# A depthwise convolution over time, moved onto the tensor engine as products over (phase, channel) rows

## The chip, the cores and the metric

The kernel runs on one core of a Trainium2 chip as a single launch. A core has a tensor engine (PE, with PEld for its weight loads), a vector engine (DVE), a scalar engine (ACT), a general engine (POOL) and a queue engine (SP) that starts the DMAs; each runs its own list of instructions in order, and they wait for each other by semaphores. Arrays live in SBUF as 128 partitions by so many elements, and the results of PE land in PSUM, from which DVE and ACT read them. The metric is device time in microseconds (us), the median of several runs.

## The reference

A decoder trunk of four layers works on 512 prompt tokens and 8 sample tokens of 1024 channels. Layer i uses token mixer i mod 3, so that the third layer alone is a convolution module; every mixer and every feed-forward block has a norm before and after it and is added to the running state x.

```
def conv_mixer(h, hist, w_in, b_in, w_dw, b_dw, ln_g, ln_b, w_out, b_out):
    a = h @ w_in + b_in                                  # 1024 -> 2048
    u = a[..., :D_MODEL] * jax.nn.sigmoid(a[..., D_MODEL:])
    uh = jnp.concatenate([hist, u], axis=1)              # 30 tokens of history, zeros for the prompt
    c = conv_general_dilated(uh, w_dw[:, None, :], feature_group_count=D_MODEL, ...) + b_dw   # 31 taps
    mu, var = mean and variance of c over the channels
    z = (c - mu) * lax.rsqrt(var + LN_EPS) * ln_g + ln_b
    y = jax.nn.silu(z) @ w_out + b_out
    return y, uh[:, -CONV_HIST:]
```

The depthwise convolution is the line that matters: each channel of a token is the sum of 31 weights, one per step back in time, times the same channel of the token and the 30 before it.

## The kernel before, in words

All activations are kept with channels on partitions: eight blocks of 128 channels, each a row of 520 tokens (8 sample tokens and 512 of the prompt). The tokens are worked on in two column groups, CA (columns 0 to 263, the sample tokens and 256 of the prompt) and CB (264 to 519). Full products (`mm3`, lines 393 to 395) are three reduced-precision passes over a high and a low part of activations (`mh`, `ml`) and weights (`wh`, `wl`): three PE instructions per 128 inputs. A weight block of 128 outputs is one 512 KB DMA from SP's queue (L354), one ACT cast to `wh` (L364) and one DVE subtraction to `wl` (L365).

The convolution stage (`_conv`) walks over m = 0 to 3; each m makes two blocks of 128 channels (2m and 2m+1), for CA and then for CB. `in_products` issues 48 PE instructions for the first block of a pair, 48 for the second, and after each 48 takes up to 32 steps (`FILL_CONV`) of a generator called `fill`. Then `evac` multiplies the sums by the norm's factor (L1184, L1186, on DVE), takes the sigmoid (L1185, ACT) and writes u (L1190, L1193, DVE) into `conv_u`, where each block has 30 zero tokens ahead of 512.

The generator holds the depthwise convolution of the two blocks of the m before. `depthwise` divides the 31 taps by the table `CONV_TAPS`: for blocks 0 to 5, over all 512 tokens, 15 on DVE (L1272, L1274, each a multiply and add in place over `y`), 11 on ACT as products (L1263) that POOL adds up (L1268), and 5 on PE (L1249) with a diagonal 128 by 128 matrix that ACT makes for each tap (L1248). The three partial sums meet on DVE (L1278, L1279). Blocks 6 and 7 come last and are done in halves of 256 tokens (14, 7 or 8, and the rest on PE). `sum_blocks` (L1293) then makes the sums over the channels with a matrix of ones, `layer_norm` (L1306 to L1321) subtracts the mean, squares, forms the factor (`rstat`, L179 to L186), multiplies by it, applies the SiLU and splits into `mh` and `ml`, and `linear_out` multiplies by `conv_w_out`. The norm of CA runs beside the taps of blocks 6 and 7 for the second half. `conv_out` (L1230 to L1232) transposes the last 30 tokens of u and the sample tokens and writes them out.

The program text gives one order per engine; a static scheduler then reorders instructions by its own estimates, with the limits of the tile pools (so many buffers of a name) and the dependencies. At the start of the stage the previous block's tail is still in progress: for CB, DVE makes `xt` (L234), POOL adds it to x (L239), ACT and DVE split it into `mh` and `ml` (L318, L319), and the products of m = 0 for CB wait for that.

## Times and the profile before

| | us |
|---|---|
| median of 3 runs | 2636.73 (2634.72 to 2644.44) |
| profiled execution | 2639.77 |
| its span on the core | 2638.0 |
| mean granted TensorE clock, share of full speed | 0.973 |
| PE busy over the span | 2490.6 (94%) |
| DVE busy | 1764.8 (67%) |
| ACT busy | 1326.9 (50%) |
| POOL busy | 503.1 (19%) |

The rest of the profiled execution, 1.8 us, lies outside the span. Busy shares are averages over the whole program; the stage of the convolution is a small part of it, from about 1513 us of the span (the first product of `conv_w_in`) to about 1776 (the last one of `conv_w_out` for CA is close by). In rows of products a record begins when its first column enters and its end is modelled, so that records overlap: the time one product costs is the step from one start to the next.

### The profile page before, as it was taken

How to read it: one execution, taken by the hardware profiler on the slowest of the kernel's cores; microseconds unless marked ns; L12 is line 12 of the kernel's file. 1: busy time of each engine (PE TensorE's matmuls, PEld its weight loads, DVE VectorE, ACT ScalarE, POOL GpSimd, SP SyncE). 2: the span in 40 equal slices, each digit the busy share in tenths (PEclk: the TensorE clock that was granted, in tenths of full speed). 3: DMA queues.
4: the chain of work that ended last, by engine and by line, in shares of the span. 5: the costliest groups of instructions: out<-in, count | busy, mean ns of one | idle time of the engine just before them, and what ended most of it. 6: DMA issues, size and time to landing. Idle time of an engine off the chain costs nothing. (4 is left out here: it accounts for less than half of the span.)

```text
span 2638.0 us, 50548 instructions
## 1 busy us (share of the span) xinstructions
PE 2490.6 (94%) x20200; PEld 2437.6 (92%) x20200; DVE 1764.8 (67%) x3063; ACT 1326.9 (50%) x2484; POOL 503.1 (19%) x667
## 2 busy tenths in 40 slices
PE   7999999999999999899999996679999998999998
PEld 7899999999999998799999984579999998999998
DVE  5745555677887777676555599977646456746464
ACT  6634334566666556554433464466534236644342
POOL 3100002233233332310000256622000005200002
PEclk8999999999999999999999998789999998999999
DMA  4575553444444444446555320025646442556451
GB/s 144 161 215 158 152 152 108 128 125 140 137 140 135 122 137 139 133 143 186 157 153 150 98 73 17 18 65 138 193 142 184 120 124 65 158 165 174 136 160 57
DMA packets 653432, 349.76 MB, mean 133 GB/s; under 512 B 14864, under 2 KB 649729, under 8 KB 652909
## 3 DMA queue, kind: packets, MB, share of 16 engines
q1 hardware_dynamic: 648996, 338.10, 44.8%
q0 software_dynamic: 1232, 6.06, 0.8%
q8 instruction: 159, 2.61, 0.4%
q10 hardware_dynamic: 2969, 2.37, 0.4%
q14 instruction: 76, 0.62, 0.1%
HBM read 331.87 MB, written 20.68 MB: 134 GB/s over the span
## 5 line engine op out<-in xcount | busy, mean ns | idle before, releaser
L393 PE MATMUL mm<-mh,wh 128*128 128x264 f32 (+1 forms) x4544 | 1310.6, 290 | 34.9 <-DVE u L1184 19.7
L394 PE MATMUL mm<-ml,wh 128*128 128x264 f32 (+1 forms) x4544 | 1295.5, 285 | 6.5 <-DVE ml L319 6.0
L395 PE MATMUL mm<-mh,wl 128*128 128x264 f32 (+1 forms) x4544 | 1291.3, 285 | 1.1 <-DVE wl L365 1.1
L364 ACT CAST wh<-raw 128x1024 fp32r<-128x1024 f32 (+1 forms) x557 | 574.0, 1036 | 655.6 <-PE mm L394 391.7
L393 PEld LDWEIGHTS mm<-mh,wh 128*128 128x128 f32 x4544 | 864.9, 191 | 41.9 <-DVE u L1184 21.6
L365 DVE TENSOR_TENSOR wl<-raw,wh 128x1024 fp32r<-128x1024 f32 (+1 forms) x557 | 691.9, 1246 | 284.1 <-ACT wh L364 281.8
L394 PEld LDWEIGHTS mm<-ml,wh 128*128 128x128 f32 x4544 | 868.0, 191 | 12.4 <-DVE ml L319 10.1
L395 PEld LDWEIGHTS mm<-mh,wl 128*128 128x128 f32 x4544 | 866.6, 191 | 1.6 <-DVE wl L365 1.5
L393 PE MATMUL mm<-h,wh 128*128 128x264 f32 (+1 forms) x1408 | 399.9, 284 | 1.0 <-DVE pr L1159 0.8
L394 PE MATMUL mm<-h,wh 128*128 128x264 f32 (+1 forms) x1408 | 399.0, 283 | 1.0 <-DVE h L422 0.9
L395 PE MATMUL mm<-h,wl 128*128 128x264 f32 (+1 forms) x1408 | 399.1, 283 | 0.0
L222 POOL TENSOR_TENSOR acc<-acc,sq 128x264 f32<-128x264 f32 (+1 forms) x90 | 78.5, 872 | 1389.9 <-ACT sq L221 1386.8
L393 PEld LDWEIGHTS mm<-h,wh 128*128 128x128 f32 x1408 | 266.4, 189 | 2.2 <-issue 1.0
L394 PEld LDWEIGHTS mm<-h,wh 128*128 128x128 f32 x1408 | 266.5, 189 | 1.7 <-DVE h L422 1.4
L395 PEld LDWEIGHTS mm<-h,wl 128*128 128x128 f32 x1408 | 266.3, 189 | 0.1
L419 DVE TENSOR_TENSOR u<-mm,r 128x264 f32<-128x264 f32 (+1 forms) x176 | 74.9, 425 | 84.9 <-PE mm L395 84.8
L1274 DVE SCALAR_TENSOR_TENSOR y<-conv_u,vec,y 128x512 f32<-128x512 f32 (+1 forms) x136 | 131.3, 1001 | 0.0
L239 POOL TENSOR_TENSOR x<-x,xt 128x264 f32<-128x264 f32 (+1 forms) x111 | 98.0, 906 | 96.3 <-DVE xt L234 94.6
L1268 POOL TENSOR_TENSOR tapa<-tapa,tapp 128x512 f32<-128x512 f32 (+1 forms) x76 | 105.5, 1388 | 18.3 <-DVE y L1279 12.5
L456 DVE TENSOR_TENSOR y<-mm,y 128x264 f32<-128x264 f32 x64 | 24.0, 429 | 124.5 <-PE mm L395 124.5
L417 DVE TENSOR_TENSOR g<-mm,r 128x264 f32<-128x264 f32 (+1 forms) x176 | 74.8, 425 | 41.6 <-PE mm L395 37.7
L937 ACT ACTIVATE x<-x,own 128x256 f32<-128x256 f32 (+1 forms) x128 | 62.6, 490 | 63.4 <-DVE own L936 62.4
(223 smaller groups left out, 2688.2 us busy)
## 6 DMA issues: line engine op xcount, KB each, us to landing
raw<-in_w_ffn_in_dram SPq DMA_DIRECT2D x352, 512.0 KB
raw<-in_w_qkv_dram SPq DMA_DIRECT2D x72, 512.0 KB
raw<-in_w_ffn_out_dram SPq DMA_DIRECT2D x64, 512.0 KB
skv<-in_cache_swa_g_dram SPq DMA_DIRECT2D x32, 512.0 KB
raw<-in_w_ffn_out_dram SPq DMA_DIRECT2D x32, 384.0 KB
out_dram<-tm SPq DMA_DIRECT2D x32, 256.0 KB
raw<-in_conv_w_in_dram SPq DMA_DIRECT2D x16, 512.0 KB
skv<-in_cache_swa_g_dram SPq DMA_DIRECT2D x16, 256.0 KB
```

Of the source, the lines that this page charges most:

```text
L222: (eng or nc.vector).tensor_add(post[c], post[c], sq)
L239: self.added = nc.gpsimd.tensor_add(xb, xb, t)
L364: whi = nc.scalar.copy(wh, raw)
L365: self.parted = whi, nc.vector.tensor_sub(wl, raw, wh.bitcast(F32))
L393: nc.tensor.matmul(ps, wh[:, k, :], mh, start=first, stop=False)
L394: nc.tensor.matmul(ps, wh[:, k, :], ml, start=False, stop=False)
L395: nc.tensor.matmul(ps, wl[:, k, :], mh, start=False, stop=last)
L417: nc.vector.tensor_mul(g, pg[2 * i], rr[c])
L419: nc.vector.tensor_mul(u, pg[2 * i + 1], rr[c])
L937: nc.scalar.activation(pc, pc, AF.Exp, scale=-1.0, bias=stat[:, lay, 0, c:c + 1], accum_out=stat[:, lay, 1, c:c + 1])
L1268: nc.gpsimd.tensor_add(a2, ap, pr)
L1274: nc.vector.scalar_tensor_tensor(yb, win(ub, t), wd[:, b, t:t + 1], yb, op0=ALU.mult, op1=ALU.add)
```

## The change

The taps of DVE, ACT and POOL go; PE does all 31 for all eight blocks. A block's u is stored by phase, that is by token number mod 4 (`cu`: phase p, then 128 tokens n, with token 4n + p), and POOL copies it (`to_phases`) into four tiles, one for each group q of 32 channels, whose 128 rows are 4 phases by 32 channels; eight zero columns stand ahead. A weight matrix of 128 by 128 then holds, for a step of m columns (4m tokens) back, the taps between each of the four input phases and each of the four output phases; nine such steps cover the 31 taps. A group is therefore nine products of 128 columns summed in PSUM, a block 4 x 9 = 36. The matrices are cut out of one tile `dg` of 128 x 36 x 32 per group, which DVE makes (L1241) by multiplying an identity pattern by the weights of `w2`; `w2` and the biases `b2` are laid out once by POOL (`depthwise_setup`). Sixteen instructions of 32 partitions by 2 x 64 bring a block from PSUM to `y`, with the bias, back on its channel rows but with the prompt tokens of each column group by phase; for blocks 0 to 5 all are ACT's, for blocks 6 and 7 every second one is DVE's. The multiplication by the norm's factor puts the tokens back in order (two instructions for CA instead of one). `CONV_FILL` says how many steps of six products are taken after each 48 products. The taps of the last m and all channel sums now come after the loop.

```diff
-FILL_CONV = 32
-CONV_TAPS = [(15, 11), (14, 7), (14, 8)]
+CONV_FILL = {(1, CB): 3, (2, CA): 3, (2, CB): 3, (3, CA): 3, (3, CB): 2}
...
-            if fill:
-                for _ in range(FILL_CONV):
-                    next(fill, None)
+            for _ in range(n_fill):
+                next(fill, None)
...
-        nc.gpsimd.memset(u[:, :, 0:H], 0.0)
...
+        self.u2 = [lp.tile([128, 4, 8 + 128], F32, name=f"conv_u2{i}") for i in range(4)]
+        self.depthwise_setup(lp)
...
+        fill = chain(*(self.depthwise(lp, b) for b in range(NB)))
...
-                            nc.vector.scalar_tensor_tensor(u[:, b, H:H + 256], a[:, NS:], self.v(R_BIN, b), g[:, NS:],
-                                                           op0=ALU.add, op1=ALU.mult)
...
+                            ub[b] = lp.tile([128, 4, 128], F32, tag="cu", name=self.n("cu"), bufs=4)
+                        o, n0 = (NS, 0) if lo == 0 else (0, 64)
+                        phases = lambda x: x[:, o:].rearrange("c (n p) -> c p n", p=4)
+                        nc.vector.scalar_tensor_tensor(ub[b][:, :, n0:n0 + 64], phases(a), self.v(R_BIN, b), phases(g),
+                                                       op0=ALU.add, op1=ALU.mult)
+                        if lo > 0:
+                            self.to_phases(b, ub[b])
+
+                self.in_products(ww, c, rr, evac, fill, CONV_FILL.get((m, c), 0))
             self.flush()
-            for _ in fill:
-                pass
-            if m < 3:
-                fill = chain(*(self.depthwise(lp, b, 0, SEQ, CONV_TAPS[0]) for b in (2 * m, 2 * m + 1)))
-            if m > 1:
-                for s in sums:
-                    for _ in range(2):
-                        next(s)
+        for _ in fill:
+            pass
+        for s in sums:
+            for _ in range(7):
+                next(s)
         self.conv_out(j)
         norm = [self.layer_norm(c, s) for c, s in zip((CA, CB), sums)]
-        for _ in chain(*(self.depthwise(lp, b, 0, 256, CONV_TAPS[1]) for b in (6, 7))):
+        for _ in norm[0]:
             pass
...
+    def depthwise_setup(self, lp):
+
+        nc = self.nc
+        self.w2 = lp.tile([128, NB, 4, 36], F32, name="conv_w2")
+        self.b2 = lp.tile([128, NB, 4], F32, name="conv_b2")
+        self.id32 = lp.tile([128, 32], F32, name="conv_id")
+        nc.vector.tensor_reduce(self.id32, self.ident.rearrange("p (b k) -> p k b", b=4), axis=AX.X, op=ALU.add)
+        nc.gpsimd.memset(self.w2, 0.0)
+        for u2 in self.u2:
+            nc.gpsimd.memset(u2[:, :, 0:8], 0.0)
+        for p in range(4):
+            for q in range(4):
+                pp, pq = slice(32 * p, 32 * p + 32), slice(32 * q, 32 * q + 32)
+                nc.gpsimd.tensor_copy(self.w2[pp, :, q, 5 - p:36 - p], self.vec[pq, :, R_DW:R_DW + 31])
+                nc.gpsimd.tensor_copy(self.b2[pp, :, q], self.vec[pq, :, R_BDW])
+
+    def to_phases(self, b, ub):
+
+        nc, u2 = self.nc, self.u2[b % 4]
+        for q in range(4):
+            for p in range(4):
+                nc.gpsimd.tensor_copy(u2[32 * p:32 * p + 32, q, 8:], ub[32 * q:32 * q + 32, p, :])
+        nc.gpsimd.tensor_copy(self.ul[:, b, :].rearrange("c (n p) -> c p n", p=4), ub[:, :, 120:128])
+
+    def depthwise(self, lp, b):
...
+        for q in range(4):
+            d = lp.tile([128, 36, 32], F32, tag="dg", name=self.n("dg"), bufs=6)
+            nc.vector.tensor_mul(d, self.id32[:, None, :].to_broadcast([128, 36, 32]),
+                                 self.w2[:, b, q, :, None].to_broadcast([128, 36, 32]))
+            dg.append(d)
+        ps = self.psum()
+        for q in range(4):
+            for m in range(9):
+                nc.tensor.matmul(ps[:, q * 128:q * 128 + 128], dg[q][:, 32 - 4 * m:36 - 4 * m, :].rearrange("p e c -> p (e c)"),
+                                 u2[:, q, 8 - m:136 - m], start=m == 0, stop=m == 8, skip_group_check=True)
+                if (q * 9 + m) % 6 == 5:
+                    yield
+        yb = self.y[:, b, NS:].rearrange("c (h p n) -> c h p n", h=2, p=4)
+        for q in range(4):
+            for s in range(4):
+                src = ps[32 * s:32 * s + 32, q * 128:q * 128 + 128].rearrange("c (h n) -> c h n", h=2)
+                dst, bias = yb[32 * q:32 * q + 32, :, 3 - s, :], self.b2[32 * s:32 * s + 32, b, q:q + 1]
+                if b >= 6 and s % 2:
+                    nc.vector.tensor_scalar(dst, src, bias, None, op0=ALU.add)
+                else:
+                    nc.scalar.activation(dst, src, AF.Identity, bias=bias)
```

Removed with it (not shown): the old `depthwise`, its halves for blocks 6 and 7, and `self.u`. After the scheduler, three places read as follows. A row is the instruction's number on its engine, its line, the operation, and tile names with their numbers; xN is a run of equal rows. Line numbers are each kernel's own (L239 before is L238 after).

On POOL, at the start of the stage, before:

```order
202 L239 TENSOR_TENSOR x<-x,xt_18721 128x264
203 L239 TENSOR_TENSOR x<-x,xt_18726 128x264
204 L1170 MEMSET conv_u 128x8x30
205 L177 MEMSET sd_19013 128x1
206 L239 TENSOR_TENSOR x<-x,xt_18899 128x256
207 L239 TENSOR_TENSOR x<-x,xt_18904 128x256
208 L239 TENSOR_TENSOR x<-x,xt_18909 128x256
209 L239 TENSOR_TENSOR x<-x,xt_18914 128x256
210 L239 TENSOR_TENSOR x<-x,xt_18919 128x256
```

And after, where the rows from 204 on are the two kinds of memset and sixteen pairs of copies, and these are the last two pairs:

```order
237 L1223 COPY conv_w_18796<-vec 32x8x31
238 L1224 COPY conv_b_18797<-vec 32x8
239 L1223 COPY conv_w_18796<-vec 32x8x31
240 L1224 COPY conv_b_18797<-vec 32x8
241 L176 MEMSET sd_19057 128x1
242 L238 TENSOR_TENSOR x<-x,xt_18943 128x256
243 L238 TENSOR_TENSOR x<-x,xt_18948 128x256
244 L238 TENSOR_TENSOR x<-x,xt_18953 128x256
245 L238 TENSOR_TENSOR x<-x,xt_18958 128x256
```

The 37 rows of the setup stand ahead of the eight additions to x of column group CB.

On DVE, at the same place (with what each row waits for), before:

```order
1808 L365 TENSOR_TENSOR wl_19173<-raw_19170,wh_19172 128x1024 [waits DMAHW3_49,Activation_49]
1809 L333 TENSOR_TENSOR acc_2643_18867<-acc_2643_18867,sq_18875 128x264 [waits DVE_49]
1810 L184 RECIPROCAL rd_18895<-sd_18891 128x2 [waits Activation_49]
1811 L333 TENSOR_TENSOR acc_2643_18867<-acc_2643_18867,sq_18878 128x264 [waits DVE_49]
1812 L333 TENSOR_TENSOR acc_2643_18867<-acc_2643_18867,sq_18881 128x264 [waits DVE_49]
1813 L234 SCALAR_TENSOR_TENSOR xt_18899<-mm_18890,vec,y 128x256 [waits PE_49]
1814 L333 TENSOR_TENSOR acc_2643_18867<-acc_2643_18867,sq_18884 128x264 [waits DVE_49]
1815 L234 SCALAR_TENSOR_TENSOR xt_18904<-mm_18890,vec,y 128x256
```

And after:

```order
1808 L331 TENSOR_TENSOR acc_2643_18911<-acc_2643_18911,sq_18916 128x264 [waits DVE_49,Activation_49]
1809 L183 RECIPROCAL rd_18939<-sd_18935 128x2 [waits Activation_49]
1810 L363 TENSOR_TENSOR wl_19253<-raw_19250,wh_19252 128x1024 [waits DMAHW3_49]
1811 L331 TENSOR_TENSOR acc_2643_18911<-acc_2643_18911,sq_18919 128x264 [waits DVE_49]
1812 L1241 TENSOR_TENSOR dg_19434<-conv_id,conv_w_18796 128x1152 [waits Pool_49]
1813 L331 TENSOR_TENSOR acc_2643_18911<-acc_2643_18911,sq_18922 128x264 [waits DVE_49]
1814 L233 SCALAR_TENSOR_TENSOR xt_18943<-mm_18934,vec,y 128x256 [waits PE_49]
1815 L331 TENSOR_TENSOR acc_2643_18911<-acc_2643_18911,sq_18925 128x264 [waits DVE_49]
```

The first weight matrix (L1241, row 1812) waits for POOL and stands ahead of the first `xt` of CB (L234 before, L233 after).

On PE, at the end of the stage, before (L1249 are taps of block 7's second half; L1293 the channel sums of CB; L393 the first product of `linear_out`):

```order
12340 L1249 MATMUL mm_20596<-conv_u,dg_20612 128x256
12341 L1249 MATMUL mm_20596<-conv_u,dg_20615 128x256
12342 L1249 MATMUL mm_20596<-conv_u,dg_20618 128x256
12343 L1249 MATMUL mm_20596<-conv_u,dg_20621 128x256
12344 L179 MATMUL mm_20655<-ones,acc_3014_20624 128x2 x2
12345 L179 MATMUL mm_20655<-ones,acc_3014_20624 8x2
12346 L1293 MATMUL mm_19971<-y,ones 128x256 x3
12347 L186 MATMUL mm_20655<-ident,rd_20663 128x128 x2
12348 L186 MATMUL mm_20655<-ident,rd_20663 128x8
12349 L393 MATMUL mm_20812<-mh,wh_20802 128x264
12350 L393 MATMUL mm_20813<-mh,wh_20808 128x264
12351 L393 MATMUL mm_20916<-mh,wh_20906 128x264
```

And after (L1247 are the last three of block 7's four groups of products; L1282 the sums, L1272 the transposes of `conv_out`):

```order
12297 L1247 MATMUL mm_20551<-conv_u_18795,dg_20545 128x128 x9
12298 L1247 MATMUL mm_20551<-conv_u_18795,dg_20547 128x128 x9
12299 L1247 MATMUL mm_20551<-conv_u_18795,dg_20549 128x128 x9
12300 L1282 MATMUL mm_20606<-y,ones 128x264 x7
12301 L1282 MATMUL mm_20614<-y,ones 128x256 x7
12302 L1272 MATMUL mm_20623<-ident,conv_us 8x128 x4
12303 L1272 MATMUL mm_20629<-ident,conv_us 8x128 x4
12304 L1272 MATMUL mm_20637<-ident,conv_ul 32x128 x4
12305 L1272 MATMUL mm_20643<-ident,conv_ul 32x128 x4
12306 L1282 MATMUL mm_20606<-y,ones 128x264
12307 L1282 MATMUL mm_20614<-y,ones 128x256
12308 L178 MATMUL mm_20682<-ones,acc_2832_20651 128x2 x2
```

The taps of blocks 4 to 7 (24 + 36 + 36 + 36 products) end in one run, then come the sums with all but the last block, the transposes, and the sums' last product; the products of CB's half no longer stand between the sums of CA and the norm.

## Rows read from the trace of the kernel before

**Rows 1.** Windows of the conv stage: busy time per engine, PEclk, DMA share, GB/s.
```profile
1513.40:1550.40 37.00, 33.66 (x271) 32.44 (x269) 32.76 (x72) 27.72 (x58) 8.84 (x14) 1.00 0.46 129
1550.40:1724.90 174.50, 120.52 (x669) 97.20 (x670) 174.04 (x212) 82.72 (x169) 118.98 (x86) 0.85 0.06 17
```

**Rows 2.** Waits, 1550.4 to 1724.9: us in total, times, longest us.
```profile
PE mm L393 <- DVE u L1184: 19.7, 3, 9.4
...
PE mm L1249 <- DVE conv_u L1193: 9.7, 2, 9.0
```

**Rows 3.** Lines by form, DVE, 1550.4 to 1743.3: busy us, mean ns.
```profile
L1274 DVE SCALAR_TENSOR_TENSOR y<-conv_u,vec,y 128x512 f32<-128x512 f32 x84 | 103.4, 1260 | 0.0
...
L1306 DVE SCALAR_TENSOR_TENSOR y<-mm,y 128x264 f32<-128x264 f32 x8 | 2.9, 424 | 0.6 <-PE mm L1293 0.6
```

**Rows 4.** Timeline, DVE: start us, us, line, count.
```profile
1553.78 15.34 DVE L1274 SCALAR_TENSOR_TENSOR y<-conv_u,vec,y 128x512 f32<-128x512 f32 x9
...
1637.41 0.73 DVE L1274 SCALAR_TENSOR_TENSOR y<-conv_u,vec,y 128x512 f32<-128x512 f32 x1
...
1642.94 2.29 DVE L365 TENSOR_TENSOR wl<-raw,wh 128x1024 fp32r<-128x1024 f32 x1
```

**Rows 5.** Timeline, POOL, same stretch.
```profile
1553.65 14.92 POOL L1268 TENSOR_TENSOR tapa<-tapa,tapp 128x512 f32<-128x512 f32 x9
```

**Rows 6.** Timeline, PE: products of 264 and of 256 tokens.
```profile
1513.44 0.28 PE L393 MATMUL mm<-mh,wh 128*128 128x264 f32 x1
...
1516.12 0.29 PE L394 MATMUL mm<-ml,wh 128*128 128x264 f32 x1
...
1540.73 0.28 PE L393 MATMUL mm<-mh,wh 128*128 128x256 f32 x1
...
1542.71 0.28 PE L395 MATMUL mm<-mh,wl 128*128 128x256 f32 x1
```

**Rows 7.** Timeline, PE: products with a fresh weight tile each.
```profile
22.74 2.04 PE L615 MATMUL mm<-bands,h 128*128 128x144 f32 x16
```

**Rows 8.** Windows around such products, at two clocks.
```profile
19.40:21.40 2.00, 2.00 (x10) 2.00 (x10) 0.01 (x1) 0.36 (x2) 0.00 (x0) 0.50 0.24 72
22.80:24.70 1.90, 1.90 (x17) 1.78 (x16) 0.88 (x2) 1.76 (x4) 0.00 (x0) 1.00 0.34 95
```

**Rows 9.** Lines, PE, 1513.4 to 1550.38.
```profile
L393 PE MATMUL mm<-mh,wh 128*128 128x264 f32 (+1 forms) x80 | 23.0, 288 | 0.0
```

**Rows 10.** One line, POOL: ns min/median/max.
```profile
L975 POOL COPY oth<-own x128: 180/186/1251, 535.5 to 1058.1; 32x4 f32<-32x4 f32 x128
```

**Rows 11.** Lines by form, POOL, whole span.
```profile
L1085 POOL TENSOR_TENSOR skv<-skv,y 128x1152 f32<-128x1152 f32 x16 | 43.0, 2707 | 24.0 <-DMA skv<-scr 23.4
```

**Rows 12.** Timeline, POOL, 1512 to 1536.
```profile
1515.46 0.29 POOL L1170 MEMSET conv_u<- 128x240 f32 x1
...
1524.19 3.15 POOL L239 TENSOR_TENSOR x<-x,xt 128x256 f32<-128x256 f32 x4 [8.40 <-DVE xt L234]
```

**Rows 13.** Timeline, DVE, 1520 to 1527.
```profile
1523.62 0.48 DVE L234 SCALAR_TENSOR_TENSOR xt<-mm,vec,y 128x256 f32<-128x256 f32 x1
```

**Rows 14.** One line, ACT: ns min/median/max.
```profile
L1248 ACT ACTIVATE dg<-ident,vec x68: 384/387/402, 1520.5 to 1731.7; 128x128 f32<-128x128 f32 x68
```

**Rows 15.** One line, DVE: ns min/median/max.
```profile
L1159 DVE TENSOR_TENSOR pr<-mm,vec x16: 269/273/275, 1180.8 to 1223.2; 128x120 f32<-128x120 f32 x16
```

**Rows 16.** Timeline, PE, 1722 to 1745.4.
```profile
1723.70 1.25 PE L1293 MATMUL mm<-y,ones 128*128 128x264 f32 x2 [6.27 <-DVE y L1279]
...
1735.98 0.70 PE L179 MATMUL mm<-ones,acc 128*128 128x2 f32 x6 [1.07 <-DVE acc L1312]
...
1743.36 1.03 PE L393 MATMUL mm<-mh,wh 128*128 128x264 f32 x3 [3.30 <-ACT mh L1321]
```

**Rows 17.** Timeline, SP queue, 1695 to 1752.
```profile
1707.93 1.30 SPq L1232 DMA_DIRECT2D out_dram<-raw  x2
1709.79 41.32 SPq L354 DMA_DIRECT2D raw<-in_conv_w_out_dram  x7
```

More of the change, by code (lines that the diff above doesn't have):

```diff
@@ L1206, in _conv @@
+        for s in sums:
+            for _ in range(7):
+                next(s)
         self.conv_out(j)
         norm = [self.layer_norm(c, s) for c, s in zip((CA, CB), sums)]
-        for _ in chain(*(self.depthwise(lp, b, 0, 256, CONV_TAPS[1]) for b in (6, 7))):
+        for _ in norm[0]:
             pass
-        self.run(self.late)
-        for _ in sums[0]:
-            pass
-        half = [self.depthwise(lp, b, 256, SEQ, CONV_TAPS[2], True) for b in (6, 7)]
-        for h in half:
-            next(h)
@@ L1216, in _conv @@
-        for _ in chain(norm[0], *half):
-            pass
-        self.run(self.late)
         post = self.post(lambda b: self.v(post_row, b))
         self.linear_out(I["conv_w_out"][j], post, next_row, bias_row=R_BOUT, between=norm[1])
+    def depthwise_setup(self, lp):
[12 more added lines that the diff above has]
+                nc.gpsimd.tensor_copy(self.b2[pp, :, q], self.vec[pq, :, R_BDW])
@@ L1231, in conv_out @@
                 nc.scalar.copy(o[:n, hb * 512:(hb + 1) * 512], ps[:n, :])
-            nc.sync.dma_start(dst, o[:n, :])
-    def depthwise(self, lp, b, t0, t1, split, early=False):
-        nc, u, us = self.nc, self.u, self.us
-        wd = self.vec[:, :, R_DW:R_DW + 31]
-        n = t1 - t0
-        nd, npl = split
-        yb = self.y[:, b, NS + t0:NS + t1]
-        win = lambda x, t: x[:, t:t + n]
-        ub = u[:, b, t0:t1 + CONV_HIST]
-        td, tpl, tpe = range(nd), range(nd, nd + npl), range(nd + npl, 31)
-        ps, ap = self.psum(128, n), None
-        def on_pe(t):
-            dg = lp.tile([128, 128], F32, tag="dg", name=self.n("dg"), bufs=8)
-            nc.scalar.activation(dg, self.ident, AF.Identity, scale=wd[:, b, t:t + 1])
-            nc.tensor.matmul(ps, dg, win(ub, t), start=t == tpe[0], stop=t == tpe[-1])
-        if early:
-            for t in tpe:
-                on_pe(t)
-            yield
-        for i in range(0, 64):
-            if i == 24:
-                self.run(self.late)
-            now = lambda r: [t for k, t in enumerate(r) if k * 64 // len(r) == i]
-            for t in () if early else now(tpe):
-                on_pe(t)
-            for t in now(tpl):
-                pr = lp.tile([128, SEQ], F32, tag="tapp", name=self.n("tapp"), bufs=10)[:, :n]
-                nc.scalar.activation(pr, win(ub, t), AF.Identity, scale=wd[:, b, t:t + 1])
-                if ap is None:
-                    ap = pr
-                else:
-                    a2 = lp.tile([128, SEQ], F32, tag="tapa", name=self.n("tapa"), bufs=4)[:, :n]
-                    nc.gpsimd.tensor_add(a2, ap, pr)
-                    ap = a2
-            for t in now(td):
-                if t == 0:
-                    nc.vector.tensor_scalar(yb, win(ub, 0), wd[:, b, 0:1], self.v(R_BDW, b), op0=ALU.mult, op1=ALU.add)
-                else:
-                    nc.vector.scalar_tensor_tensor(yb, win(ub, t), wd[:, b, t:t + 1], yb, op0=ALU.mult, op1=ALU.add)
-            yield
-        def finish():
-            nc.vector.tensor_add(yb, yb, ps)
-            nc.vector.tensor_add(yb, yb, ap)
-            if t0 == 0:
-                ys = self.y[:, b, 0:NS]
-                nc.vector.tensor_scalar(ys, us[:, b, :], wd[:, b, 30:31], self.v(R_BDW, b), op0=ALU.mult, op1=ALU.add)
-                nc.vector.tensor_add(ys, ys, self.conv_cs[:, b, :])
-        self.late.append(finish)
@@ L1287, in sum_blocks @@
+            nc.sync.dma_start(dst, o[skip:n, :])
     def sum_blocks(self, c):
```

29 lines of the change are left out of this document (16 added, 13 removed).

## The prediction

> **What bounds the kernel now.** I read the windows of the conv stage first, then the waits inside it, then the lines and the timeline of the engine that was waited for. PE is 94% busy over the whole span, so this change can only matter where PE is not. The windows show the place: from 1550.4 to 1724.9, 174.5 us, DVE is busy 174.04 us, PE only 120.52 at a granted clock of 0.85, POOL 118.98; in the 37 us ahead of it PE is busy 33.66 us at clock 1.00 [rows 1]. The waits name DVE: PE stood 19.7 us at the first product after an evacuation and 9.7 us at the taps [rows 2]. On DVE the taps hold the time: 84 of them over 512 tokens took 103.4 us, a mean of 1260 ns [rows 3]. One beside no POOL work takes 0.73 us; nine in a row beside POOL's additions took 15.34 us, 1.70 each, and POOL's nine took 14.92 [rows 4, 5]. The two engines hold each other up. So in this stretch DVE is the bound, with POOL as its brake, and PE is what runs over as soon as DVE is let off.
>
> **What it removes.** All of L1274, L1272, L1268 and L1263, the diagonals, and the finishing additions. With them DVE's bound goes. What is late next is PE itself, and its time is a sum of products.
>
> **PE's sum, step by step.** The products of conv_w_in stay: 768, half of 264 columns at (1516.12 - 1513.44)/22 = 0.122 us, half of 256 at (1542.71 - 1540.73)/17 = 0.1165 us [rows 6]; 384 x 0.122 + 384 x 0.1165 = 91.5 us. Taps: 8 blocks x 36 = 288 products of 128 x 128. A full-precision product leaves two records (block taps: 68 products, 136 records), so 576 records. The nearest row is L615, sixteen records of 128 and 144 columns with a fresh weight tile each: 2.04 us, or (2.04 - 0.28)/15 = 0.117 each without the modelled tail of the last [rows 7]; for 128 columns instead of 136 on average that is 0.117 x 128/136 = 0.11, which I take: 63.4 us. The ends are 0.10 and 0.1275 (2.04/16): 58 and 73 us.
>
> Before 1550.4 the stage also held 7.6 us of other things: 37.0 us up to the first tap, of which 240 products (80 each of three lines [rows 9]) are 144 x 0.122 + 96 x 0.1165 = 28.8 and the small norm products and waits the rest (36.3 to 1549.7). They stay.
>
> **POOL's setup in front of CB.** POOL's rows show 1 + 4 memsets and 16 pairs of copies ahead of CB's additions to x, and DVE's rows show the first dg, which waits for them, ahead of the first xt. Before, POOL was free at 1515.8 and its first addition began at 1524.19 [rows 12], after xt at 1523.62 [rows 13]. No row shows these copies. A copy of 32 x 4 takes 186 ns at the median and 1251 at most [rows 10]; the memset of 240 elements took 0.29 us [rows 12]; an addition of 1152 elements takes 2.71 us, 2.35 ns per element [rows 11]. So a copy of 248 elements costs between 0.19 and 0.19 + 0.58 = 0.77; I take 0.45, the middle, and 0.19 for the small one. 16 x 0.64 = 10.2, plus 1.4 (1152 elements by the memset) and 0.4: 12 us, from 7 to 17. Setup ends at 1527.5. Then dg: 1152 elements by L365's 1024 in 1.15 us [rows 4] is 1.3 us. The first xt starts at 1528.8 instead of 1523.62: +5 us (0 to 11), and behind it stand xt, x, the split and m = 0's products for CB, with PE having nothing else ready. Cost 5 us.
>
> **End of the dense part.** 1513.4 + 91.5 + 63.4 + 7.6 + 5 = 1680.9.
>
> **The engines beside it.** One m is now 192 product records (22.9 us) and 144 tap records (15.8 us): 38.7 us of PE. In it DVE has 8 dg x 1.3 = 10.4, four wl x 1.15 and fourteen evacuation operations of about 0.42 (as the subtractions in rows 3), some 21 us. ACT has 32 evacuations; the nearest row is a 128 x 128 activation, 387 ns [rows 14]: 12.4 us, with casts and sigmoids about 20. POOL has 2 x 17 copies of 128 elements, between 0.19 and 0.49 each, say 0.34: 11.6 us. All three are hidden with nearly half the stretch to spare. The narrowest place is the end: the last conv_w_in product comes 132 tap products, 29 us, before the end of the dense part, at 1652; with some 3 us of evacuation block 6 and 7 can be copied from 1655 on, in 34 x 0.34 = 11.6 us, and block 7's products start at 1680.9 - 7.9 = 1673. At 0.49 each it would be 1671.7, still in time.
>
> **The tail.** Block 7's sixteen evacuations alternate between ACT and DVE, each row with a wait for the other: 8 x 0.387 + 8 x 0.273 (128 x 120 out of PSUM, L1159 [rows 15]) = 5.3, and sixteen handovers, which no row prices; I allow 0.1 each: 7 us (4 if both engines run side by side, 9 with 0.2 each). The transposes of conv_out run under it. A last sum, 0.6. Then the norm of CA: before, from the end of its sums at 1724.95 to the first product of conv_w_out at 1743.36 it took 18.4 us, because DVE had taps between; from L179 at 1735.98 on it is 7.4 us [rows 16]. Without taps the first part is eight subtractions of 0.424 [rows 3] and about two more operations of that size: 4.3 us. 4.3 + 7.4 = 11.7, rounded to 12. First product: 1680.9 + 7 + 0.6 + 12 = 1700.5, which is 42.9 us ahead of 1743.36. The weights allow it: SP's loads 2 to 8 of conv_w_out stand behind conv_out's DMA, which came at 1707.93 [rows 17] and now follows the transposes, at about 1690. From there on nothing changes.
>
> **Sum.** -43, less about 1 for a PE that idles longer in the tail (some 20 us, before 5 to 8 at a time) and comes back at the lower clock: -42. Against the profiled run's own 2639.77 that is 2597.8; the median of before lies 3 us lower, 2636.73, which gives 2594.7. I predict 2596.
>
> **A page that speaks against it.** DVE and POOL in lock-step is in rows 4 and 5, while L365, also with both inputs in SBUF, ran at 1.15 us beside POOL in the same stretch, as fast as alone [rows 4]: not every such instruction is slowed. The Trainium skill, SBUF — State Buffer, section "Who interferes with whom", has it as an exclusive lock: a DVE instruction with two SBUF inputs holds off a GpSimd instruction that reads SBUF, and the other way round. By it the 32 dg (41 us) and the wl would stand against the 136 copies; the 15 us per m that DVE spends on them would come on top of POOL's 11.6, still under 38.7. At the narrow place some six dg would put 8 us on 1666.6, 2 us past 1673: -40 instead of -42. The taps' rows agree with it, L365's do not, and the sum stays.
>
> **Rivals.**
>
> *POOL sets the pace (the other side).* The copies of a block must be in u2 before PE can start it. If a copy costs c, block 7 is ready at 1655 + 34c if POOL has kept up until then, and at 1555 + 136c if it has not (before, the first tap at 1550.4 [rows 1] had waited for block 0's u, which now comes 5 us later). Up to c = 0.53 nothing shows; from there each 0.1 us costs 3.4, and from 0.98 on, where the second line passes the first, 13.6. At 1.18 the gain of 42 is gone (2638), from 1.28 on the kernel is slower by over 13 us, and at 1.5 it ends at 2682. For it: L975 reached 1.251 us, seven times its median [rows 10]. Against: that median is 0.186, and a copy has one input where L1085 has two.
>
> *The clock.* From 19.4 to 21.4 us the granted clock was 0.50, its lower level (1.2 GHz), and ten such records fell in 2.00 us, 0.20 each; from 22.8 it was 1.00 and seventeen fell in 1.90, 0.11 each; PE was busy all of both [rows 8]. Taps at 0.22 throughout would cost 63 us more (2659); a third of them 21 (2617). For it: before's stretch at 0.85. Against: that stretch had PE waiting for DVE, and the 37 us before it, with PE 91% busy, had 1.00 [rows 1].
>
> *The front and the tail cost more.* Setup 17 us, handovers 0.2, and the norm as slow as before: +6, +2, +6, with the clock in the tail +4: 2614. In the other direction, setup hidden under m = 0's CA products (-5), evacuation side by side (-3), and taps at 0.10 (-6): 2582.
>
> **Chances.** My forecast with its own range of 2584 to 2612: 0.68. A dear front and tail, still faster: 0.12. POOL's pace: 0.10, of which 0.02 still faster, 0.05 level, 0.03 slower. The clock: 0.10, of which 0.03 faster, 0.03 level, 0.04 slower. Faster or slower by over 0.5%, 13 us, is what a measurement here can tell from no change: faster 0.85, within 0.08, slower 0.07. The range for 8 in 10 is the forecast's with the dear front and tail: 2582 to 2622.
>
> **What will show it.** Right: DVE's busy share near a half between 1550 and 1680; the tap records (L1247) 0.11 us apart at clock near 1.0, in one unbroken run at the end; the first product of conv_w_out near 1701. The front step: idle time of DVE ahead of the first dg, ended by POOL, and xt of CB about 5 us later. The tail: ACT and DVE taking turns at L1257 and L1259 for about 7 us with PE idle. Wrong: copies of L1231 near 1 us and PE's taps waiting for POOL; tap records 0.2 apart; or a first product of conv_w_out that comes after 1715.

## The result, and the profile after

The changed kernel takes 2593.5 us (median of 4 runs, 2591.78 to 2596.35) against 2635.72 for the kernel before on the same chip: a ratio of 0.9843, with a 95% interval of 0.9828 to 0.9858, or 42 us less. 2596 was predicted, with 42 us less as the sum. The gain came out nearly to the microsecond; the terms did not, and the errors on both sides nearly cancelled.

Since the two profiled executions also differ by some microseconds far from the change (the stage's first product starts at 1513.44 before and 1510.58 after; the last stretch, from 300 products into the feed-forward block to PE's last product, took 787.2 and 785.7), the places below are counted from the stage's own first product, by the starts of PE's products in the timelines:

| us after the first product of conv_w_in | before | after |
|---|---|---|
| m = 0, CB begins | 14.6 | 21.8 |
| m = 2, CA begins | 64.0 | 67.9 |
| m = 3, CA begins | 120.3 | 106.9 |
| last product of conv_w_in begins | 177.5 | 140.5 |
| first product of conv_w_out | 229.9 | 193.4 |
| conv_w_out, CA done | 262.5 | 221.3 |
| first product of the feed-forward block | 286.7 | 245.6 |

The windows of the kernel after (columns as in [rows 1]) answer to [rows 1]:

```profile
1510.60:1552.00 41.40, 33.71 (x259) 32.93 (x258) 33.84 (x65) 23.09 (x46) 23.98 (x50) 0.92 0.28 77
1552.00:1680.70 128.70, 128.70 (x1117) 128.70 (x1116) 72.50 (x107) 50.58 (x124) 66.05 (x136) 1.00 0.09 26
1680.70:1703.90 23.20, 11.80 (x62) 9.76 (x60) 16.19 (x42) 16.44 (x33) 2.22 (x3) 0.76 0.36 97
1703.90:1740.00 36.10, 35.50 (x270) 35.27 (x271) 22.23 (x43) 29.01 (x65) 7.63 (x10) 0.92 0.30 88
```

From 1552 to 1680.7 PE is busy all of 128.70 us at a granted clock of 1.00 (before: 120.52 of 174.5 at 0.85), and DVE 72.50 us of it, 56%. The bound has gone from DVE to PE. What is not PE's lies at both ends: 7.7 us in the first window, 11.4 in the third. The waits of PE over the stage (us in total, times, longest) have no taps and no evacuation any more [rows 2], and name those two ends:

```profile
PE mm L178 <- DVE acc L1301: 7.1, 2, 6.6
PE mm L178 <- DVE acc L331: 5.6, 1, 5.6
PE mm L185 <- DVE rd L183: 4.2, 4, 2.1
PE mm L391 <- ACT mh L1315: 4.0, 1, 4.0
```

The first and second are the norm of the convolution and the squares of the block before; none is POOL's copies. PE's timeline at the end of the stage answers to [rows 16] (start, us, instruction, count, idle time before it):

```profile
1651.23 29.64 PE L1247 MATMUL mm<-conv_u,dg 128*128 128x128 f32 x264
1680.71 6.30 PE L1282 MATMUL mm<-y,ones 128*128 128x264 f32 x28
1686.85 1.04 PE L1272 MATMUL mm<-ident,conv_us 128*8 128x128 f32 x8
...
1688.60 1.04 PE L1282 MATMUL mm<-y,ones 128*128 128x264 f32 x4
1696.22 1.11 PE L178 MATMUL mm<-ones,acc 128*128 128x2 f32 x6 [6.58 <-DVE acc L1301]
...
1703.93 0.81 PE L391 MATMUL mm<-mh,wh 128*128 128x264 f32 x2 [4.00 <-ACT mh L1315]
```

The 132 products of the last taps, 264 records, run in one piece, (29.64 - 0.28)/263 = 0.112 us apart, as L615's seventeen did in [rows 8] (0.11 was predicted). Then come 7 + 7 channel sums, 6.3 us, the transposes, the last sums, and the gap of the norm.

The front: POOL, then DVE (timelines), beside [rows 12, 13]:

```profile
1516.32 1.29 POOL L1223 COPY conv_w<-vec 32x248 f32<-32x248 f32 x1
...
1521.42 0.38 POOL L1223 COPY conv_w<-vec 32x248 f32<-32x248 f32 x1
...
1529.02 1.40 POOL L238 TENSOR_TENSOR x<-x,xt 128x256 f32<-128x256 f32 x2
```

```profile
1516.15 1.21 DVE L363 TENSOR_TENSOR wl<-raw,wh 128x1024 fp32r<-128x1024 f32 x1
...
1525.27 1.36 DVE L1241 TENSOR_TENSOR dg<-conv_id,conv_w 128x1152 f32<-128x1152 f32 x1 [3.94 <-POOL conv_w L1223]
...
1527.09 0.47 DVE L233 SCALAR_TENSOR_TENSOR xt<-mm,vec,y 128x256 f32<-128x256 f32 x1
```

The same copy of 248 elements took 1.29 us when DVE worked on wl (1.21 us, both inputs in SBUF) and 0.38 when DVE stood idle. The first dg waited 3.94 us for POOL, and CB's first xt came at 1527.09, 16.5 us after the stage's first product, where before it was 10.2 [rows 6, 13]. The addition to x on POOL, which needs that xt, began only at 1529.02: the rest of the setup, up to 1528.84, stood ahead of it in POOL's own queue.

### The profile page after: what moved, and what is told of

Its sections match the earlier page's. It is cut to its first block, busy times and chain, and to the rows that moved or that the text cites. A ratio compares the mean times of both kernels' runs of the same rounds, so it can differ in the third digit from the quotient of the medians.

```text
span 2590.0 us, 51324 instructions
## 1 busy us (share of the span) xinstructions
PE 2486.6 (96%) x20640; PEld 2458.6 (95%) x20640; DVE 1666.3 (64%) x2954; ACT 1293.8 (50%) x2432; POOL 466.5 (18%) x753
## 4 chain that ended last, share of the span: by engine, by line
PE 46%; POOL 2%; DVE 1%; ACT 1%; DMA 1%; issue 1%; DVEq 0%; ACTq 0%; POOLq 0%; SPq 0%
PE mm L391 14%; PE mm L392 14%; PE mm L393 14%; PE mm L1247 2%; DMA raw<-in_w_ffn_in_dram 1%; POOL x L238 1%; DVE wl L363 0%; POOL acc L221 0%; POOL conv_w L1223 0%; ACT wh L362 0%; PE mm L185 0%; PE mm L178 0%; PE mm L1282 0%; PE mm L613 0%; ACT sq L220 0%
## 5 line engine op out<-in xcount | busy, mean ns | idle before, releaser
L393 PE MATMUL mm<-mh,wl 128*128 128x264 f32 (+1 forms) x4544 | 1285.7, 283 | 0.7 <-DVE wl L363 0.7
L393 PEld LDWEIGHTS mm<-mh,wl 128*128 128x128 f32 x4544 | 861.3, 190 | 1.0 <-DVE wl L363 0.9
L393 PE MATMUL mm<-h,wl 128*128 128x264 f32 (+1 forms) x1408 | 397.9, 283 | 0.0
L393 PEld LDWEIGHTS mm<-h,wl 128*128 128x128 f32 x1408 | 265.1, 188 | 0.1
L238 POOL TENSOR_TENSOR x<-x,xt 128x264 f32<-128x264 f32 (+1 forms) x111 | 97.6, 904 | 83.5 <-DVE xt L233 81.7
L415 DVE TENSOR_TENSOR g<-mm,r 128x264 f32<-128x264 f32 (+1 forms) x176 | 75.0, 426 | 42.8 <-PE mm L393 38.7
L1114 POOL TENSOR_TENSOR skv<-skv,lg 128x576 f32<-128x576 f32 (+1 forms) x48 | 52.5, 1126 | 219.8 <-ACT lg L1107 219.8
L418 DVE TENSOR_TENSOR u<-u,g 128x264 f32<-128x264 f32 (+1 forms) x176 | 75.8, 434 | 20.9 <-ACT g L416 7.1
```

The lines of the kernel that those rows point to most:

```text
L238: self.added = nc.gpsimd.tensor_add(xb, xb, t)
L393: nc.tensor.matmul(ps, wl[:, k, :], mh, start=False, stop=last)
L415: nc.vector.tensor_mul(g, pg[2 * i], rr[c])
L418: nc.vector.tensor_mul(u, u, g)
L1114: nc.gpsimd.tensor_mul(v4[:, :, h, :], v4[:, :, h, :], lg[:, h, o:o + n, None].to_broadcast([128, n, 64]))
```

## The experiments

Eight of the ten kernels were timed in three rounds and two in one, each against the kernel before on the same chip; where a few microseconds matter, the places in the stage are compared besides.

**Was it the new form of the products, or POOL's going?** Two variants of the kernel before keep its diagonal products and take POOL out of the convolution.

```diff
-CONV_TAPS = [(15, 11), (14, 7), (14, 8)]
+CONV_TAPS = [(26, 0), (21, 0), (22, 0)]      # the one: POOL's taps to DVE
+CONV_TAPS = [(20, 0), (17, 0), (17, 0)]      # the other: divided between DVE and PE
...
-            nc.vector.tensor_add(yb, yb, ap)
+            if ap is not None:
+                nc.vector.tensor_add(yb, yb, ap)
```

Expected of the first:

> The kernel before, with the taps of ACT and POOL (11, 7 and 8 a block) given to DVE: 26, 21 and 22 taps on DVE, 5, 10 and 9 on PE, none on POOL. Theory (POOL's additions and DVE's taps held each other up, 1.70 us each beside one another and 0.73 alone): a tap on DVE costs 0.70 throughout, 26 x 0.70 = 18.2 us a block against 15 x 1.26 = 18.9 and the finishing addition; the time stays within 15 us of the kernel before. Rival (1.26 us is what a tap costs on DVE, and POOL's share is a true saving): 11 x 1.26 us more a block, 80 to 100 us slower.

Measured: 2618.98 us, a ratio of 0.9937 (0.9918 to 0.9956): 17 us faster than before, a little more than the 15 of the theory, with seven to eleven taps a block more on the engine that was the bound. The DVE taps by lines (busy us, mean ns), against 103.4 us and 1260 ns for 84 of them in [rows 3]:

```profile
L1274 DVE SCALAR_TENSOR_TENSOR y<-conv_u,vec,y 128x512 f32<-128x512 f32 x150 | 104.5, 745 | 0.0
```

150 taps take what 84 took. POOL's and ACT's share had been worth less than nothing: an addition on POOL cost the DVE tap beside it about one microsecond (1.70 against 0.73), more than a tap on DVE takes. That is the lock-step of [rows 4, 5], now with its price in time. (conv_w_out's first half became 18.6 us longer here than in the kernel after, 46.5 against 27.9, since CB's taps of blocks 6 and 7 stand on DVE beside it.)

Expected of the second:

> The kernel before, with ACT's and POOL's taps divided between DVE and PE: 20, 17 and 17 taps on DVE, 11, 14 and 14 on PE with diagonal matrices as before, none on POOL. Theory (DVE bound, PE with room, POOL a brake): DVE's taps fall from 131 to about 113 us and the finishing additions go, PE's rise by 38 us into its idle time; the time falls by 10 to 26 us. Rival (it is the form of the products that brings the gain, and diagonal ones only move the bound to PE): no change or slower.

Measured: 2592.65 us, 0.9839 (0.9818 to 0.986), 44 us faster than before, where 10 to 26 were expected, and level with the change itself, 2593.5. The forecast was too careful: I had DVE's taps at 113 us (80.2 + 28.2 = 108.4 were measured), and did not count the clock, which was 0.85 before in the stretch with PE waiting [rows 1] and is 1.00 here. The window of its taps:

```profile
1545.00:1690.00 145.00, 144.20 (x780) 108.78 (x780) 139.38 (x270) 55.20 (x133) 0.28 (x1) 1.00 0.12 35
```

PE is busy 144.20 of 145 us at clock 1.00 and DVE 139.38: both are full. The DVE taps from 1540 to 1730 (busy us, mean ns):

```profile
L1274 DVE SCALAR_TENSOR_TENSOR y<-conv_u,vec,y 128x512 f32<-128x512 f32 x114 | 80.2, 743 | 0.1
L1274 DVE SCALAR_TENSOR_TENSOR y<-conv_u,vec,y 128x256 f32<-128x256 f32 x64 | 28.2, 478 | 0.5
```

So the gain does not need rows of phase and channel. It needs POOL out of DVE's way and some 80 us of taps on PE (its diagonal products were busy 58.7 us over 512 tokens and 24.5 over 256).

**What the new form is for.** All taps but one of each block on PE, with diagonals.

```diff
+CONV_TAPS = [(1, 0), (1, 0), (1, 0)]
```

> The kernel before, with all taps but the first of each block on PE as products with a diagonal matrix (30 of 512 columns a block instead of 36 of 128): what the move to PE costs without the rows of phase and channel. 240 products of 512 tokens (block 6 and 7 in halves), 0.434 x 2 = 0.87 us each, are 208 us against 64: the first product of conv_w_out at 320 to 345 us of the stage, the time 2720 to 2750, slower than before by some 90 to 110. Rival (PE's time for such a product is set by its weights, not its columns, so that both forms cost alike): about 2610.

Measured: 2718.52 us, 1.0329 (1.0276 to 1.0382), the first product of conv_w_out at 320.2 us, both about at the lower edge of what was expected. The time of these full-precision products goes by their columns: a record of 512 took 0.435 us here (156.6 us for 360) and one of 256 took 0.218 (52.2 for 240), one of 128 in the kernel after 0.112. 30 x 512 columns a block against 36 x 128 is a factor of 3.3, and PE alone is the bound:

```profile
1550.00:1800.00 250.00, 250.00 (x1048) 159.20 (x1047) 41.35 (x84) 108.90 (x268) 0.00 (x0) 1.00 0.09 26
```

The phase form is what lets PE take all 31 taps for 64 us; a mixture with DVE does as well as long as DVE has room.

**The front: is it the order in the queues?** The setup is put behind CB's additions to x.

```diff
-        self.depthwise_setup(lp)
...
                 self.in_products(ww, c, rr, evac, fill, CONV_FILL.get((m, c), 0))
+                if m == 0 and c == CA:
+                    with self.behind((self.added,)):
+                        self.depthwise_setup(lp)
```

> The kernel after, with the setup of w2, b2 and the zero columns placed behind the additions to x of column group CB on POOL, so that the first dg no longer stands ahead of xt on DVE. Theory (the front step is a matter of order in the two queues): the wait of PE for the sums of squares, 5.59 us, and most of the 2.06 us one go; products of m = 0 for CB start as in the kernel before, the first product of conv_w_out comes 5 to 8 us earlier against the stage's first product (193.35 us now, 186 to 188 then), and the time is 5 to 8 us below the kernel after, about 2587. Rival (the front is lost to the lock between POOL's copies and DVE, wherever they stand, or the setup is then late for block 0): the stage stays within 2 us of 193.35.

Measured: 2590.91 us, 0.9832 (0.9816 to 0.9848), 2.6 us below the kernel after and within the intervals of both. The first half of the theory held: m = 0 for CB begins at 14.6 us as before. Then it was given back: m = 2 begins at 66.6, and the first product of conv_w_out at 191.9, 1.5 us earlier, where 5 to 8 had been expected: the setup was late for block 0, as the rival had it. DVE's timeline shows the new wait:

```profile
1549.76 1.36 DVE L1243 TENSOR_TENSOR dg<-conv_id,conv_w 128x1152 f32<-128x1152 f32 x1 [3.20 <-POOL conv_w L1225]
...
1558.68 1.27 DVE L1190 SCALAR_TENSOR_TENSOR cu<-g,vec,u 128x256 f32<-128x256 f32 x2
```

Four dg stand one after another for POOL's setup, ahead of u of CB, which comes at 1558.68, and POOL's copies of block 0 wait for that. A second version puts them behind it:

```diff
+            with self.behind((self.cu,) if b == 0 else ()):     # cu: u of block 1, CB
+                nc.vector.tensor_mul(d, self.id32[:, None, :].to_broadcast([128, 36, 32]), ...)
```

> As the run with the setup behind the additions to x, and block 0's four weight matrices put on DVE behind u of blocks 0 and 1 (CB), since there they had waited for POOL's setup (3.2 us and more) ahead of u, and had held back u, POOL's copies and PE's first taps. Theory (the front's 7 us were won and given back at that one wait): products of m = 0 for CB 14.6 us after the stage's first product as in that run, those of m = 2 at about 61 to 63 instead of 66.64, the first product of conv_w_out at 186 to 188 (193.35 in the kernel after). Rival (POOL with setup and copies is itself late, since DVE's two-input instructions hold it off): m = 2 stays at 65 or later, and the first product of conv_w_out at 190 or later.

Measured: 2586.97 us, 0.9815 (0.9794 to 0.9836); m = 2 at 61.5, the first product of conv_w_out at 186.9, as expected. PE's waits over the stage (to be read beside the kernel after's, above):

```profile
PE mm L178 <- DVE acc L1306: 7.2, 2, 6.6
PE mm L391 <- ACT mh L1320: 3.9, 1, 3.9
PE mm L185 <- DVE rd L183: 2.9, 4, 0.9
```

The wait for the squares, 5.6 us, is gone. The front was a matter of order, at two places.

**The tail: what sets it?** Each group of 32 channels is evacuated right behind its nine products, on ACT alone.

```diff
         for q in range(4):
             for m in range(9):
                 nc.tensor.matmul(ps[:, q * 128:q * 128 + 128], ...)
+            for s in range(4):
+                ...
+                nc.scalar.activation(dst, src, AF.Identity, bias=bias)
```

> The kernel after, with each group of 32 channels brought from PSUM right behind its own nine products, all by ACT, instead of sixteen instructions behind the block's last product (alternating with DVE for blocks 6 and 7). Theory A (the serial evacuation of 6.2 us after the last tap sets the tail): the last sum of CA comes 4 to 5 us earlier after the last tap (8.9 us now), and so does the first product of conv_w_out. Theory B (PE's own work there, 28 sum records in 6.30 us and the transposes in 1.9, is as long as the evacuation, so that it hides it): under 1 us.

Measured: 2604.61 us, 0.9885 (0.987 to 0.99), 11 us slower than the kernel after, which neither theory had. A wait that was not there before shows:

```profile
PE mm L1248 <- ACT y L1255: 6.2, 14, 0.9
```

The four groups share one PSUM tile, and PE's next group now waits until ACT has read the last: the shown waits are 6.2 us, and the last product of conv_w_in begins at 147.2 instead of 140.5, with 57.7 instead of 52.8 us from there to conv_w_out. With the sums of CB and the transposes behind CA's sums as well:

```diff
-        for s in sums:
-            for _ in range(7):
-                next(s)
-        self.conv_out(j)
+        for _ in range(7):
+            next(sums[0])
         norm = [self.layer_norm(c, s) for c, s in zip((CA, CB), sums)]
+        next(norm[0])
+        self.conv_out(j)
+        for _ in range(7):
+            next(sums[1])
```

> As the run with evacuation by group, and besides the channel sums of CB and the transposes of conv_out behind those of CA, in the time of the norm, where PE stood idle for 6.6 us. By theory B the two together are what counts: PE has about 2 us of transposes and one sum left after the last tap, the last sum of CA comes about 3 us after it instead of 8.9, and the first product of conv_w_out 5 to 6 us earlier than in the kernel after: about 2588. By theory A evacuation alone did it already, and this run gains nothing over that one.

Measured: 2603.99 us, 0.9876 (0.986 to 0.9893), not the 2588 expected. The step from the last product of conv_w_in to conv_w_out is 55.2 us, 2.5 less than without the move of the sums, but the waits of PE for ACT remain. Counted from the last tap, though, the pair shows what the tail is made of: conv_w_out begins 23.2 us after its end in the kernel after, 19.4 with evacuation by group and 16.9 with the sums moved as well, and the last sum of CA ends 8.9, 5.4 and 2.3 us after it. So the order of PE's own work counts, as theory B had it. What the two runs lost lies ahead of the last tap: from the last product of conv_w_in to it they took 38.1 us, not 29.5, with some of the waits and with sums that had moved in between the taps of block 7.

**Both ends mended.** The front's second version, CA's sums first, and for blocks 6 and 7 a PSUM tile for each group:

```diff
+        late = b >= 6
+        pss = [self.psum(128, 128) for _ in range(4)] if late else [self.psum()] * 4
...
+            if late:
+                out(q)
```

> The run before this one, and for blocks 6 and 7 a PSUM tile for each group of 32 channels (so that PE's next group need not wait for ACT's reading of the last, as it did in the run with evacuation by group: 6.2 us in 14 waits), evacuation by group on ACT alone, and the sums of CB and the transposes behind those of CA. Theory: after the last tap PE has only CA's eight sums, of which the last waits some 2 us for ACT; the last sum of CA is 4 to 5 us after the last tap instead of 8.9, and the first product of conv_w_out comes at 181 to 184 us of the stage: about 2583. Rival (ACT is the bound of the tail): the tail stays as it is, and the run equals the one before.

Measured: 2582.59 us, 0.9799 (0.9778 to 0.982): the fastest of all, 11 us below the change. The first product of conv_w_out comes at 180.3 us, 6.6 earlier than with the front's second version alone. Its tail:

```profile
1676.54 3.73 PE L1296 MATMUL mm<-y,ones 128*128 128x264 f32 x16
1680.10 1.04 PE L1286 MATMUL mm<-ident,conv_us 128*8 128x128 f32 x8
...
1681.84 3.62 PE L1296 MATMUL mm<-y,ones 128*128 128x256 f32 x16
1686.75 0.70 PE L178 MATMUL mm<-ones,acc 128*128 128x2 f32 x6 [1.28 <-DVE acc L1315]
...
1693.69 0.59 PE L391 MATMUL mm<-mh,wh 128*128 128x264 f32 x1 [3.55 <-ACT mh L1329]
```

From the last tap to the last sum of CA it is now 3.7 us, not 8.9; the transposes and CB's sums fill what was the gap. The taps up to the last one take 29.5 us again and show no wait for ACT. Part of the gain went again: conv_w_out's first half took 30.5 us, not 27.9, so that 4.0 of the 6.6 us were left at the feed-forward block. (This run changes the place of the evacuation, the PSUM tiles and the order of the sums at once; their shares were not taken apart here.)

**The clock in the gap.** 28 products nobody reads between CA's last sum and the norm's small products, and 16 behind those.

```diff
+        if c == CA:
+            self.stir(28)
...
+        if c == CA:
+            with self.behind((self.spread,)):
+                self.stir(16)
```

> The kernel after, with 28 products of a matrix of ones whose result nobody reads between CA's last sum and the norm's small products, and 16 behind those: PE is busy through the two gaps of 6.6 and 4.0 us. Theory (PE comes back from the gaps at the lower clock): the products of conv_w_out, which are 0.22 us apart for the first 6 us in the kernel after, are 0.12 apart from the first on; linear_out's first half ends about 3 us earlier, the time is 2 to 4 us lower. Rival (the clock falls for another reason, or the added products delay the norm's small ones by as much): within 1 us.

Measured: 2593.71 us, 0.9841 (0.9827 to 0.9856), level with the kernel after, so that in time the rival was right. The windows of the gap and of conv_w_out's first part, and below them the kernel after's window of the same length:

```profile
1680.50:1705.10 24.60, 22.25 (x149) 20.26 (x149) 15.68 (x44) 16.87 (x36) 2.24 (x3) 0.93 0.27 72
1705.10:1725.00 19.90, 18.67 (x155) 18.50 (x154) 13.93 (x27) 18.07 (x38) 5.54 (x7) 1.00 0.55 158
```

```profile
1703.90:1723.80 19.90, 19.30 (x134) 19.12 (x135) 13.47 (x26) 16.99 (x35) 5.82 (x7) 0.85 0.46 136
```

With the gap filled the granted clock is 1.00 behind it, without 0.85, and conv_w_out's first half takes 26.0 us instead of 27.9. But the first product comes 1.5 us later: the 16 products took 5.2 us, more than the gap of 4.0. What an idle gap costs in clock is shown, about 2 us here; this filling gave it back.

**POOL's room.** Each copy into the four tiles is made twice.

```diff
-                nc.gpsimd.tensor_copy(u2[32 * p:32 * p + 32, q, 8:], ub[32 * q:32 * q + 32, p, :])
+                for _ in range(2):
+                    nc.gpsimd.tensor_copy(u2[32 * p:32 * p + 32, q, 8:], ub[32 * q:32 * q + 32, p, :])
```

> The kernel after, with each of the 128 copies of to_phases issued twice (the second writes the same values again): POOL's work on them doubles. Theory, from the trace of the kernel after: in the middle of the stage the copies have room, but block 0's took 11.55 us and block 1's 10.33, beside DVE's two-input instructions, and ended 2 us ahead of need; doubled, block 1 is ready some 13 us late, block 7 a few: m = 3 starts 12 to 18 us later, the time is 12 to 22 us longer, about 2610. Rival (the copies are hidden, as the sum of the prediction had it, with half the stretch to spare): under 4 us longer.

Measured: 2599.11 us (2 runs), 0.9875 (0.9821 to 0.993); in the stage, the first product of conv_w_out comes 5.2 us later. Neither number was right. PE's taps now wait for POOL, and POOL's timeline shows why:

```profile
PE mm L1248 <- POOL conv_u L1232: 3.3, 6, 1.0
```

```profile
1556.67 22.80 POOL L1232 COPY conv_u<-cu 32x128 f32<-32x128 f32 x32 [16.90 <-DVE cu L1191]
...
1580.68 14.31 POOL L1232 COPY conv_u<-cu 32x128 f32<-32x128 f32 x32
...
1674.35 10.86 POOL L1232 COPY conv_u<-cu 32x128 f32<-32x128 f32 x32
```

Block 0's copies took 22.80 us and block 1's 14.31, and POOL was never idle again until block 7's ended at 1685.2. PE's order (48 products of conv_w_in between two pieces of taps) left block 1 more time than I had counted, as I read it: 1.8 us were lost up to m = 2, and 3.4 at the end, behind block 7's copies. So POOL had just under half its time to spare, as in the prediction, and no more: doubled copies are about where it begins to set the pace.

## Why the prediction was right, step by step

**The bound** was read rightly. DVE held PE up because POOL held DVE up; with the taps gone PE is busy without a gap for 128.7 us. What the prediction did not see is that this is all there is to it: taking POOL's and ACT's taps away and adding five or six a block to PE in the old form does as much.

**PE's sum** was right to 1 us. Tap records were 0.112 us apart, 576 x 0.112 = 64 us (63.4); the steps from m = 2 to m = 3 took 39.0 (38.7).

**The front** was mis-sized: 5 us predicted, 7.2 measured (21.8 against 14.6). Eleven of the sixteen copies were cheaper than thought, 0.38 to 0.40 (0.45), and one took 0.56; the small ones took 0.19 or, beside DVE, 0.40. But four of the sixteen, beside a wl or dg of DVE with two inputs in SBUF, took 1.29 to 1.48. Setup lasted from 1512.58 to 1528.8, 16.2 us instead of 12. The range given was 7 to 17. The path was not quite the predicted one either: the first dg did not wait for all of the setup (it began at 1525.27), but x did, in POOL's own queue. And behind PE's wait of 5.6 us the granted clock was 0.54 for 3.9 us (1532.3 to 1536.2), where before it was 1.00 at this place; the prediction had counted nothing for that. Half a microsecond came back: the dense part ended 170.1 us after the start, where 167.5 was predicted.

**The tail** was mis-sized, and partly for a wrong reason: 19.6 us from the last tap to conv_w_out, 23.2 measured. ACT and DVE do take turns (ACT's timeline: block 5's sixteen, all its own, then the first and the last of its eight for block 7, each after a wait for DVE or PE):

```profile
1664.83 5.93 ACT L1259 ACTIVATE y<-mm,conv_b 32x128 f32<-32x128 f32 x16 [2.11 <-PE mm L1247]
...
1680.91 0.36 ACT L1259 ACTIVATE y<-mm,conv_b 32x128 f32<-32x128 f32 x1 [2.26 <-PE mm L1247]
...
1686.34 0.36 ACT L1259 ACTIVATE y<-mm,conv_b 32x128 f32<-32x128 f32 x1 [0.41 <-DVE y L1257]
```

Sixteen in turns took 6.2 us (7 predicted), sixteen on ACT 5.93. But they were not what the last sum waited for: the evacuation ended at 1687.1, and PE itself had 7.9 us of sums and transposes ahead of CA's last sum, up to 1688.60, which the prediction took to run under the evacuation. Last tap to last sum: 8.9 us, not 7.6. The norm took 14.3 us, not 12. Most of that is its first part, up to L178: 6.6 us where 4.3 were predicted, with one weight block's wl (1.38 us) among the squares on DVE. From L178 on it took 7.7 (7.4), with three casts on ACT between the root and the SiLU. The 1 us put down for the clock behind the tail's gaps was about 2, by the run with the gaps filled.

**What cancelled it:** by the first product of conv_w_out 36.6 us had been won, not 42.9. Then conv_w_out's first half took 27.9 us instead of 32.6, a term the prediction set at nothing ("From there on nothing changes"). Before, PE waited there for CB's squares, as the timelines of before and after show:

```profile
1760.26 1.01 PE L179 MATMUL mm<-ones,acc 128*128 128x2 f32 x4 [3.18 <-DVE acc L1312]
```

```profile
1719.20 0.58 PE L178 MATMUL mm<-ones,acc 128*128 128x2 f32 x4 [0.57 <-DVE acc L1301]
```

Before, CB's subtractions of the mean came only after CB's taps on DVE; after, they are done in the norm's gap. That wait is 2.6 of the 4.7 us. Most of the rest is the stretch behind it, at a granted clock of 0.90 before and 1.00 after:

```profile
1763.00:1783.00 20.00, 20.00 (x155) 19.96 (x154) 7.38 (x19) 11.15 (x28) 1.51 (x2) 0.90 0.01 2
```

```profile
1723.00:1743.00 20.00, 20.00 (x169) 19.81 (x167) 9.43 (x20) 14.29 (x33) 2.25 (x3) 1.00 0.20 57
```

A term on the far side of the place where the sum stopped: 4.7 us. It brings the stage to 41.2 us at the start of the feed-forward block. That the gain came out at 42 is therefore luck in part: without this term it would have been some 5 us under the forecast.

**The rivals.** POOL's pace: the copies cost 0.288 us at the median, 0.34 predicted, with 1.42 at most (ns min/median/max):

```profile
L1231 POOL COPY conv_u<-cu x128: 283/288/1422, 1555.1 to 1664.4; 32x128 f32<-32x128 f32 x128
```

Per block they took 6.3 to 11.6 us, 0.72 a copy in the worst block, and PE never waited for them. At the narrow place blocks 6 and 7 took

```profile
1644.94 6.30 POOL L1231 COPY conv_u<-cu 32x128 f32<-32x128 f32 x16 [21.72 <-DVE cu L1191]
...
1653.31 11.43 POOL L1231 COPY conv_u<-cu 32x128 f32<-32x128 f32 x16 [1.76 <-DVE cu L1191]
```

that is 0.55 a copy, just over the limit of 0.53, and still ended 8 us before block 7's products: block 6's u came well before the 1655 from which the prediction let both be copied. The clock: 1.00 through the taps.

The page on SBUF: I left its lock out of the sum because L365 ran at full speed beside POOL. That was a misreading. The L365 that ran at full speed, 1.21 us, had no POOL work beside them: POOL stood idle for 14.17 us up to 1641.18. The one beside POOL's additions is the last line of [rows 4], and it took 2.29 us.

```profile
1640.12 1.21 DVE L365 TENSOR_TENSOR wl<-raw,wh 128x1024 fp32r<-128x1024 f32 x1
```

```profile
1641.18 1.28 POOL L1268 TENSOR_TENSOR tapa<-tapp,tapp 128x512 f32<-128x512 f32 x1 [14.17 <-ACT tapp L1263]
```

In the kernel after it shows on the other engine: beside a copy, wl and dg keep their 1.20 to 1.36 us, and the copy takes 1.29 to 1.48 instead of 0.38. Either engine can be the one that is late, so both have to be read. The Trainium skill (SBUF — State Buffer, "Who interferes with whom") has it as an exclusive lock in which the order of issue decides who waits. These rows agree with it: the delay falls now on DVE, now on POOL.

## What to carry to other kernels

Two engines can be slower together than one of them alone: before dividing work between DVE and POOL, price it with both running, and try the version in which POOL does nothing. When a bound is moved to PE, follow the sum past the point where the old stage ended, and count what PE itself has to do in the tail; the work of the small engines that used to stand there may be worth as much as the errors at the front. A setup that is needed late is to be placed late in the queue of every engine that touches it, and what waits for it as well.

## What the runs showed of the hardware that was not expected

A POOL copy of 32 x 248 took 0.38 us alone and 1.29 to 1.48 beside one wl or dg of DVE, with both inputs in SBUF (1.20 to 1.36 us); a wl beside POOL's additions took 2.29 us instead of 1.21. A DVE tap over 512 tokens took 0.743 us on average with POOL out of the convolution, 1.26 in the kernel before, where POOL added beside a part of them (1.70 each in a row of nine beside its additions).

Reading one group of a PSUM tile by ACT and writing the next group of the same tile by PE were ordered one behind the other and cost PE 6.2 us of shown waits, in a run that was 11 us slower in all; with a tile for each group in blocks 6 and 7, and the other blocks evacuated at their end, the wait was gone. The Trainium skill's page "PSUM — Partial Sum Buffer" (section "PSUM bank collisions raise a hardware error") says that two engines must not be on the same part of a bank at once, which would be a reason for such an order; no run here took the order away.
